# An encoder-layer kernel: start loads from two queues, two down tiles at once, another order of the last products, and some low weight parts added by transfer

## The chip, the cores and the metric

The kernel runs on one core of one Trainium2 chip. The metric is the device time of one execution in microseconds (us); before the change its median over three runs is 1635.33 us (1635.21 to 1636.85). The core has TensorE (PE in the profile; its weight loads are PEld), VectorE (DVE), ScalarE (ACT), GpSimd (POOL) and SyncE (SP); each works through its own queue of instructions in order.

## What is computed

One step of a streaming encoder layer for 512 prompt tokens and 64 sample tokens (576 in all), model width 1024, hidden width 2816:

```python
h = layer_norm(ALPHA * x + 0.5 * swiglu_ffn(x, p['ffn1_w_gu'], p['ffn1_w_down']), p['ln1_g'], p['ln1_b'])
mix, new_state = token_mixer(h, p, conv_prev, ml_state, att_past)
h = layer_norm(ALPHA * h + mix, p['ln2_g'], p['ln2_b'])
h = layer_norm(ALPHA * h + 0.5 * swiglu_ffn(h, p['ffn2_w_gu'], p['ffn2_w_down']), p['ln3_g'], p['ln3_b'])

def swiglu_ffn(x, w_gu, w_down):
    gate, up = jnp.split(x @ w_gu, 2, axis=-1)
    return (jax.nn.silu(gate) * up) @ w_down
```

The token mixer projects `h` by a wide `w_in` (among its columns attention's v, k and q, the first three taken), runs an mLSTM and a band attention, and merges both. All is float32.

## The kernel before, in words

**Split precision.** A float32 operand is split into a high part, which ACT writes by a copy that rounds (`act(hi, raw)`, line 137), and a low part, the rest, which DVE writes by a subtraction (`tt(lo, raw, f(hi), ALU.subtract)`, line 140). A product is three matmuls on PE (line 123): high by high, high by low, low by high. Weights come as tiles of 128 x 1024 (the third part of a down tile is 128 x 768).

**The weight pump.** `plan` (lines 287 to 312) lists every streamed weight tile in the order of use: first gate and up tiles `gu`, then the down tiles `dn` with three parts `c` each (`DC`: 8, 8 and 6 tiles of k), then `in` 48, 40 and 32, and so on. `pump` (line 171) loads the next tile into one of two buffers `wr` from SP's queue and splits the oldest into one of four pairs `wh`, `wl`. Some tiles next to the norms (`PIECES`, line 160) are split in two pieces of 512 columns, and of two of them (`ON_POOL`) the low part is subtracted on POOL.

**The start.** Lines 332 to 338 load the first three weight tiles in column pairs (`w0`), interleaved with the eight tiles of x, all from SP's queue; lines 367 to 376 split them in the same order: per pair of k three weight pieces and two pieces of x.

**A feed-forward part** (`ffn`, line 716). A few gate and up tiles run as plain products (`gemm`). The rest run two by two as units in the manner of Strassen (`Units`, line 582): seven products of four row blocks with combinations of the activations (`Combos.make`, line 554, buffers `tx`, `NX` of them, the rest from a common pool) and of the weights (`prep`, line 608). A unit's products are, in order: a11·b11, [the two last products of the unit before], a12·b21, s2·t2, s1·t1, s3·t3, then a22·t4 and s4·b22 within the next unit or, for the last, at the end (`run`, `finish`). Copies e1, e2, e3 of partial sums go to ACT, each ahead of the product that adds to the same bank. `tail` lets the pump go on to the down tiles; it is called between the two last products.

**The down projection** (lines 770 to 776). The 22 hidden tiles `h` are split as they are needed (`Hidden`), the first eleven into `hc`, the later ones into the left slots of `h`; `get` asks for four tiles ahead. Of eight output tiles j the first six run for both token halves together, one tile after the other; the last two run half by half. Each output tile goes to `Norm.cb`.

**The norms** (`Norm`, line 385) work by halves of the tokens. `stats` sums on PE, takes the variance on DVE and the power −1/2 on POOL (`rsqrt_cols`, line 380), makes a diagonal `dg` on DVE; `spread` multiplies it out on PE; `centre` subtracts the mean, six of eight tiles on DVE and two on POOL; `apply` scales on DVE, adds the bias on ACT and splits. Behind norm 1 stand the `in` tiles, behind norm 2 the `gu2` tiles, and in norm 1 POOL also splits the past of the attention's cache (`vc`, `kh`, `kl`).

A scheduler puts the instructions of each engine in one fixed order, by priorities (`hot`, `high_priority`) and by the program's order.

Of the kernel before, what the change touches and what calls it, by code (L numbers as in the profile page):

```python
# [81 lines left out]
def tile_layer(ctx: ExitStack, tc: tile.TileContext, ins, outs):  # L82
# [53 lines left out]
    def act(out, in_, func=AF.Copy, **kw):  # L136
        ACT.activation(out, in_, func, **kw)  # L137
# [18 lines left out]
    WARM = 8  # L156
    LAST = {1: 6, 2: 6}
    CL = {1: 2, 2: 3}
    NX = 10
    PIECES = {("gu2", 0, 0), ("gu2", 0, 1), ("gu2", 1, 0), ("gu2", 1, 1), ("in", 48), ("in", 40), ("in", 32)}  # L160
    ON_POOL = {("gu2", 0, 0), ("gu2", 1, 0)}
    CP = (6, 7)
    CPF = (4, 5, 6, 7)
    GR = 450
# [5 lines left out]
    @hot(30)  # L170
    def pump(limit=2):
        while True:
            c = wst["conv"]
            if wst["dma"] < min(len(plan), c + 2):
                i = wst["dma"]
                raws[i] = wpool.tile([P, 1024], F32, tag="wr", name=nm("wr"), bufs=2)
                src = plan[i][1]
                SP.dma_start(raws[i][:, :src.shape[1]], src)
                wst["dma"] += 1
                continue  # L180
            if c < wst["stop"] and c < wst["taken"] + limit and c < wst["done"] + NWB:
                raw = raws.pop(c)
                n = plan[c][1].shape[1]
                hi = wpool.tile([P, 1024], F32R, tag="wh", name=nm("wh"), bufs=NWB)
                if plan[c][0] == "if":

                    r3 = raw[:, :n].rearrange("p (k c) -> p k c", c=64)
                    h3 = hi.rearrange("p (k c) -> p k c", c=P)
                    act(h3[:, :, 0:64], r3)
                    tt(h3[:, :, 64:128], r3, f(h3[:, :, 0:64]), ALU.subtract)  # L190
                    parts[c] = (hi, None)
                else:
                    lo = wpool.tile([P, 1024], F32R, tag="wl", name=nm("wl"), bufs=NWB)
                    step = n if plan[c][0] not in PIECES else 512
                    for a in range(0, n, step):
                        act(hi[:, a:a + step], raw[:, a:a + step])
                        tt(lo[:, a:a + step], raw[:, a:a + step], f(hi[:, a:a + step]), ALU.subtract,
                           POOL if plan[c][0] in ON_POOL else DVE)
                    parts[c] = (hi, lo)
                wst["conv"] += 1  # L200
                continue
            return
# [35 lines left out]
    def gemm(tiles, xs, cbs, passes=NORMAL, tags=None):  # L238
# [7 lines left out]
        for p, (tl, hl) in enumerate(passes):  # L246
# [27 lines left out]
            for t in tl:  # L274
                for hf in hl:
                    cbs[t](hf, pss[t, hf][:, :HALVES[hf][1]])

    def one(key):
        return [[(key, KT)]]

# [46 lines left out]
    def load_x(hf, k0):  # L327
        t0, n = HALVES[hf]
        for k in (k0, k0 + 1):
            SP.dma_start(xr[k][:, t0:t0 + n], ins["xT"][:, k, t0:t0 + n])  # L330

    for k0 in range(0, KT, 2):
        ww = slice(k0 * P, (k0 + 2) * P)
        SP.dma_start(w0[:, 0:3:2, ww], ins["w_gu1"][0:2, :, ww].rearrange("c p n -> p c n"))
        load_x(0, k0)
        SP.dma_start(w0[:, 1, ww], ins["w_gu1"][FT, :, ww])
    for k0 in range(0, KT, 2):
        load_x(1, k0)
# [204 lines left out]
    class Combos:  # L543
# [6 lines left out]
        def tile(self):  # L550
            self.n += 1
            return slot(F32R, self.pool, "tx", bufs=NX) if self.n <= NX else slot(F32R)

        def make(self, i):
            k1, k2 = 4 + i, i
            r1, r2 = self.raw[k1], self.raw[k2]
            a, b = slice(0, HT_), slice(HT_, T)
            (h1, l1), (h2, l2) = self.xs.p[k1], self.xs.p[k2]
            d = self.b[i] = {"b11": (h1[:, a], l1[:, a]), "b21": (h2[:, a], l2[:, a]), "b22": (h2[:, b], l2[:, b])}
            tmp = self.pool.tile([P, 2, HT_], F32, tag="tt", name=nm("tt"), bufs=1)  # L560
            u, v = tmp[:, 0, :], tmp[:, 1, :]
# [12 lines left out]
            out("t1", u, -1.0, ha[:, a], la[:, a])  # L574
            out("t3", v, 1.0, ha[:, b], la[:, b])
            hb, lb = self.tile(), self.tile()
            tt(v, r2[:, b], u, ALU.subtract)
            out("t2", v, -1.0, hb[:, a], lb[:, a])
            tt(u, v, r2[:, a], ALU.subtract)
            out("t4", u, 1.0, hb[:, b], lb[:, b])  # L580

    class Units:


        def __init__(self, n, j0, hr, pool, combos):
            self.w, self.hr, self.pool, self.x = ins[f"w_gu{n}"], hr, pool, combos
            self.raw, self.ws, self.p = {}, {}, {}
            self.js = list(range(j0, FT))

        def load(self, j):  # L590
            if j >= FT:
                return
            w = self.raw[j] = self.pool.tile([P, 2048], F32, tag="wu", name=nm("wu"), bufs=2)
            SP.dma_start(w[:, 0:1024], self.w[j])
            SP.dma_start(w[:, 1024:2048], self.w[FT + j])

        def parts(self, src, small=False):
            n = 512 if small else 1024
            if small:
                hi, lo = (self.pool.tile([P, 512], F32R, tag=t, name=nm(t), bufs=1) for t in ("ah", "al"))  # L600
# [7 lines left out]
        def prep(self, j, what):  # L608
# [3 lines left out]
            if what == "a":  # L612
                p["a12"], p["a11"] = self.parts(w[:, 0:1024])
            elif what == "s":
                q = self.pool.tile([P, 2, 512], F32, tag="ws", name=nm("ws"), bufs=1)
                r = self.pool.tile([P, 2, 512], F32, tag="wt", name=nm("wt"), bufs=1)
# [28 lines left out]
        def run(self, tail):  # L645
            cur = None
            for j in self.js + [None]:
# [4 lines left out]
                    with tc.high_priority(offset=60):  # L652
                        new["E1"] = self.copy(new["X"], "e1", 1)
                if cur is not None:
                    self.finish(cur, j, tail)
# [24 lines left out]
        def finish(self, u, nxt, tail):  # L680
# [6 lines left out]
            if nxt is None:  # L687
                tail()
# [7 lines left out]
    class Hidden(Act):  # L696
# [6 lines left out]
        def upto(self, k):  # L703
            while len(self.p) <= min(k, FT - 1):
                j = len(self.p)
                pool, tag = self.pools[j >= FT // 2]
                hi, lo = (pool.tile([P, T], F32R, tag=tag, name=nm(tag), bufs=FT + (tag == "h")) for _ in range(2))
# [7 lines left out]

    def ffn(xs, n, gi, raw, final=None, prev=None):
        hh = {}
        with tc.tile_pool(name=nm("hr"), bufs=FT, side="right", reuse_waits="tile") as hr:

            def gate_cb(j):  # L720
                def cb(hf, ps):
# [17 lines left out]
            with tc.tile_pool(name=nm("sx"), bufs=1, side="right", reuse_waits="tile") as sx:  # L739
                combos = Combos(xs, raw, sx)  # L740
                un = Units(n, CL[n], hr, sx, combos)
                un.hr_done = hh.__setitem__
                j0 = CL[n]
                un.load(j0)
                un.load(j0 + 1)
# [21 lines left out]
            if final is not None:  # L767

                HALVES[:], BLOCKS[:] = HALVES_[1], BLOCKS_[1]
            with tc.tile_pool(name=nm("hc"), bufs=FT, side="right", reuse_waits="tile") as hc:  # L770
# [756 lines left out]
```

## Time and profile before

| | before |
|---|---|
| median of 3 runs | 1635.33 us (1635.21 to 1636.85) |
| profiled execution | 1635.94 us |
| its span | 1634.2 us |
| mean clock granted to TensorE | 0.988 |
| PE busy | 98% of the span |
| DVE, ACT, POOL busy | 67%, 50%, 9% |
| moved by DMA | 146.51 MB, 90 GB/s on the mean |

How to read the rows that follow: a row of a timeline has the start, the time, the engine, the line of the kernel, the operation, output and input tiles, shape, the count of instructions put together, and in brackets the idle time before it with what ended it. A row of waits has the total, the count and the longest. A row of windows has a stretch of the span, its length, and the busy time of each engine within it, then the clock granted to TensorE (1.00 is full), the busy share of the DMA engines and GB/s. A row of DMA issues ends with the us from issue to landing.

### The profile page before, as it was taken

How to read it: one execution, taken by the hardware profiler on the slowest of the kernel's cores; microseconds unless marked ns; L12 is line 12 of the kernel's file. 1: busy time of each engine (PE TensorE's matmuls, PEld its weight loads, DVE VectorE, ACT ScalarE, POOL GpSimd, SP SyncE). 2: the span in 40 equal slices, each digit the busy share in tenths (PEclk: the TensorE clock that was granted, in tenths of full speed). 3: DMA queues.
4: the chain of work that ended last, by engine and by line, in shares of the span. 5: the costliest groups of instructions: out<-in, count | busy, mean ns of one | idle time of the engine just before them, and what ended most of it. 6: DMA issues, size and time to landing. Idle time of an engine off the chain costs nothing.

```text
span 1634.2 us, 29320 instructions
## 1 busy us (share of the span) xinstructions
PE 1593.3 (98%) x11831; PEld 1567.2 (96%) x11831; DVE 1090.1 (67%) x2158; ACT 811.2 (50%) x1529; POOL 141.1 (9%) x277
## 2 busy tenths in 40 slices
PE   8999998999999999999999999999999999999997
PEld 8999998999999999999999999999999999998996
DVE  7777777535788777673656748434778777768336
ACT  6445546223566566651657466443345554545223
POOL 0000000000313323000111101002020000000001
PEclk9999999999999999999999999999989999999999
DMA  6222221224342333122222122222212222212333
GB/s 215 73 83 104 93 89 48 82 84 119 120 135 89 100 106 101 48 85 85 78 72 78 59 94 67 68 78 78 83 62 103 104 83 100 104 62 59 87 93 116
DMA packets 52320, 146.51 MB, mean 90 GB/s; under 512 B 5720, under 2 KB 16600, under 8 KB 52184
## 3 DMA queue, kind: packets, MB, share of 16 engines
q1 hardware_dynamic: 52184, 144.63, 27.3%
q8 instruction: 93, 1.52, 0.4%
q14 instruction: 43, 0.35, 0.1%
HBM read 135.37 MB, written 9.24 MB: 88 GB/s over the span
## 4 chain that ended last, share of the span: by engine, by line
PE 56%; DVE 3%; issue 1%; ACT 1%; POOL 1%; ACTq 0%; POOLq 0%; DVEq 0%
PE mm L123 51%; PE aux L123 4%; PE aux L133 1%; DVE s L140 1%; DVE h L140 0%; ACT s L137 0%; DVE wl L140 0%; DVE hc L140 0%; POOL wl L140 0%; POOL kh L147 0%; DVE s L143 0%; DVE ptl L140 0%; ACT sc L137 0%; ACT L137 0%; POOL rs L382 0%
## 5 line engine op out<-in xcount | busy, mean ns | idle before, releaser
L123 PE MATMUL mm<-s,wh 128*128 128x256 f32 (+2 forms) x3872 | 796.0, 299 | 11.4 <-ACT s L137 9.3
L123 PEld LDWEIGHTS mm<-s,wh 128*128 128x128 f32 x3872 | 624.9, 190 | 16.4 <-ACT s L137 10.1
L123 PE MATMUL mm<-s,wl 128*128 128x256 f32 (+2 forms) x1920 | 569.1, 296 | 0.0
L123 PEld LDWEIGHTS mm<-s,wl 128*128 128x128 f32 x1920 | 365.0, 190 | 0.0
L140 DVE TENSOR_TENSOR wl<-wr,wh 128x1024 fp32r<-128x1024 f32 (+2 forms) x166 | 195.9, 1183 | 186.4 <-ACT wh L137 185.8
L137 ACT ACTIVATE wh<-wr 128x1024 fp32r<-128x1024 f32 (+2 forms) x171 | 169.7, 996 | 301.5 <-PE mm L123 281.6
L123 PE MATMUL mm<-hc,wh 128*128 128x256 f32 (+1 forms) x704 | 147.7, 301 | 9.8 <-DVE hc L140 5.8
L123 PE MATMUL mm<-h,wh 128*128 128x256 f32 (+1 forms) x704 | 140.7, 294 | 0.0
L123 PEld LDWEIGHTS mm<-hc,wh 128*128 128x128 f32 x704 | 116.4, 192 | 13.2 <-DVE hc L140 8.9
L123 PE MATMUL mm<-tx,wh 128*128 128x288 f32 x624 | 128.3, 296 | 0.0
L140 DVE TENSOR_TENSOR wl<-ws,wh 128x1024 fp32r<-128x1024 f32 x39 | 47.8, 1226 | 111.1 <-ACT wh L137 111.1
L123 PEld LDWEIGHTS mm<-h,wh 128*128 128x128 f32 x704 | 112.7, 187 | 0.2
L123 PE MATMUL mm<-hc,wl 128*128 128x256 f32 (+1 forms) x352 | 105.1, 299 | 0.0
L123 PE MATMUL mm<-h,wl 128*128 128x256 f32 (+1 forms) x352 | 103.3, 294 | 0.0
L123 PEld LDWEIGHTS mm<-tx,wh 128*128 128x128 f32 x624 | 100.9, 190 | 0.0
L123 PE MATMUL mm<-tx,wl 128*128 128x288 f32 x312 | 92.8, 297 | 0.0
L137 ACT ACTIVATE wh<-ws 128x1024 fp32r<-128x1024 f32 x39 | 41.3, 1058 | 102.4 <-PE mm L123 101.7
L382 POOL TENSOR_TENSOR rs<-var,mhalf 128x2 f32<-128x2 f32 (+1 forms) x6 | 5.2, 865 | 825.0 <-DVE var L143 425.0
L123 PEld LDWEIGHTS mm<-hc,wl 128*128 128x128 f32 x352 | 67.7, 192 | 0.0
L123 PEld LDWEIGHTS mm<-h,wl 128*128 128x128 f32 x352 | 65.9, 187 | 0.0
L137 ACT ACT_TABLE_LOAD x45 | 57.7, 1283 | 5.5 <-DVE U L143 4.0
L123 PEld LDWEIGHTS mm<-tx,wl 128*128 128x128 f32 x312 | 59.1, 190 | 0.0
(282 smaller groups left out, 2864.3 us busy)
## 6 DMA issues: line engine op xcount, KB each, us to landing
wu<-in_w_gu SPq DMA_DIRECT2D x78, 512.0 KB, 4.3
wr<-in_w_in SPq DMA_DIRECT2D x72, 512.0 KB, 3.5
wr<-in_w_dn SPq DMA_DIRECT2D x40, 512.0 KB, 3.5
wr<-in_w_dn SPq DMA_DIRECT2D x20, 384.0 KB, 3.2
G<-in_rbias SPq DMA_DIRECT2D x16, 256.0 KB, 2.9
wr<-in_w_ap SPq DMA_DIRECT2D x8, 512.0 KB, 3.5
wr<-in_w_mp SPq DMA_DIRECT2D x8, 512.0 KB, 3.5
wr<-in_w_o SPq DMA_DIRECT2D x8, 512.0 KB, 3.5
```

The source lines that it names most:

```text
L123: PE.matmul(out, lhsT, rhs, start=start, stop=stop, **kw)
L133: PE.transpose(out, in_, idn)
L137: ACT.activation(out, in_, func, **kw)
L140: return (eng or DVE).tensor_tensor(out, a, b, op=op)
L382: return y, POOL.tensor_tensor(y, v, mhalf[:, :n], op=ALU.pow)
```

## The change

Four things are changed.

1. **First loads.** The tiles of x for k 0 to 3, first half, are loaded from ACT's queue; SP's queue keeps the rest.
2. **Two down tiles side by side.** The new `joined` runs output tiles 0 and 1 together over all k, their sums in two kinds of banks; the plan puts their parts in that order. The split of hidden tile 0 goes to buffers of its own (`h0`) and is asked for when unit 8 is done (the scheduler may place it earlier); its place in `hc` is given back, and seven more are asked for at the start. Weight buffers of the units are in a pool of their own (`sw`), so that the order of release fits.
3. **Order of the last products.** In the last unit a12·b21 (`first`) comes after s3·t3, ahead of a22·t4; `tail` is called where a12·b21 used to be. `make` gets priority 80 and `NX` is 8.
4. **Added by transfer.** For the tiles in `ADDED` (the six `gu2` tiles, `in` 48, 40, 32, and the six parts of the first two down tiles of both feed-forward parts: 21 in all) the low part is no longer a subtraction on DVE or POOL: ACT writes −hi into `lo`, and a DMA issued from POOL's queue reads the raw tile from memory once more and adds it to `lo`. The pieces of 512 columns are gone.

```diff
-    NX = 10
-    PIECES = {("gu2", 0, 0), ("gu2", 0, 1), ("gu2", 1, 0), ("gu2", 1, 1), ("in", 48), ("in", 40), ("in", 32)}
-    ON_POOL = {("gu2", 0, 0), ("gu2", 1, 0)}
+    NX = 8
+    NH0 = 1
+    ADDED = {(f"gu2", j, e) for j in range(3) for e in range(2)} | {("in", 48), ("in", 40), ("in", 32)} \
+        | {(f"dn{n}", j, c) for n in (1, 2) for j in range(2) for c in range(3)}
...
-                    step = n if plan[c][0] not in PIECES else 512
-                    for a in range(0, n, step):
-                        act(hi[:, a:a + step], raw[:, a:a + step])
-                        tt(lo[:, a:a + step], raw[:, a:a + step], f(hi[:, a:a + step]), ALU.subtract,
-                           POOL if plan[c][0] in ON_POOL else DVE)
+                    act(hi[:, :n], raw[:, :n])
+                    if plan[c][0] in ADDED:
+                        act(lo[:, :n], f(hi[:, :n]), scale=-1.0)
+                        POOL.dma_start(lo[:, :n], plan[c][1], accum_op=ALU.add)
+                    else:
+                        tt(lo[:, :n], raw[:, :n], f(hi[:, :n]), ALU.subtract)
...
+    def joined(keys, xs, cbs):
+        pss = {(t, hf): bank("mm" if t == 0 else "aux")[:, :HALVES[hf][1]] for t in range(2) for hf in range(2)}
+        last = len(DC) - 1
+        for c, ts_ in [(c, (0, 1)) for c in range(last)] + [(last, (0,)), (last, (1,))]:
+            ids = {t: take(keys[t][c]) for t in ts_}
+            k0, nk = DC[c]
+            for i in range(nk):
+                ww = slice(i * P, (i + 1) * P)
+                st, sp = k0 + i == 0, c == last and i == nk - 1
+                for t in ts_:
+                    wh, wl = parts[ids[t]]
+                    for hf in range(2):
+                        xh, xl = xs.get(k0 + i, hf)
+                        mm(pss[t, hf], wh[:, ww], hs(xh, hf), st, False)
+                        mm(pss[t, hf], wh[:, ww], hs(xl, hf), False, False)
+                        mm(pss[t, hf], wl[:, ww], hs(xh, hf), False, sp)
+                        od.tick()
...
-        for j in (*range(KT), *range(LAST[n], KT)):
-            for c, (k0, nk) in enumerate(DC):
-                plan.append(((f"dn{n}", j, c), ins[f"w_dn{n}"][j][:, k0 * P:(k0 + nk) * P]))
+        order = [(j, c) for c in range(3) for j in range(2)]
+        order += [(j, c) for j in (*range(2, KT), *range(LAST[n], KT)) for c in range(3)]
...
-        load_x(0, k0)
+        load_x(0, k0, ACT if k0 < 4 else SP)
...
+        @hot(80)
         def make(self, i):
...
-                Y = bank("mm")[:, :HT_]
-                self.product(Y, j, "a12", "b21", True, True)
-                with tc.high_priority(offset=60):
-                    tt(h[:, :HT_], Y, new["E1"], ALU.add)
-                    act(h[:, :HT_], h[:, :HT_], AF.Silu)
+                def first(new=new, j=j, h=h):
+                    Y = bank("mm")[:, :HT_]
+                    self.product(Y, j, "a12", "b21", True, True)
+                    with tc.high_priority(offset=60):
+                        tt(h[:, :HT_], Y, new["E1"], ALU.add)
+                        act(h[:, :HT_], h[:, :HT_], AF.Silu)
+                if j < FT - 1:
+                    first()
+                else:
+                    tail()
...
+                if j == FT - 1:
+                    first()
...
+                def hr_done(j, h):
+                    hh[j] = h
+                    if j == 8:
+                        hp_.upto(NH0 - 1)
...
-                hp_ = Hidden(hh, ((hc, "hc"), (hr, "h")))
-                hp_.upto(5)
+                hp_.pools[1] = (hc, "hc", FT - 2 * NH0)
+                hp_.spare = slot(F32R, hc, "hc", bufs=FT - 2 * NH0)
+                hp_.upto(7)
...
-                for j, hl in [(j, (0, 1)) for j in range(LAST[n])] + [(j, (hf,)) for hf in (0, 1) for j in range(LAST[n], KT)]:
+                joined([[(f"dn{n}", j, c) for c in range(3)] for j in range(2)], hp_, [ln.cb(j) for j in range(2)])
+                for j, hl in [(j, (0, 1)) for j in range(2, LAST[n])] + [(j, (hf,)) for hf in (0, 1) for j in range(LAST[n], KT)]:
```

More of the change, by code (lines that the diff above doesn't have):

```diff
@@ L276, in gemm @@
                     cbs[t](hf, pss[t, hf][:, :HALVES[hf][1]])
+    def joined(keys, xs, cbs):
[15 more added lines that the diff above has]
+                        od.tick()
+            for t in ts_:
+                done(ids[t])
+                if c == last:
+                    for hf in range(2):
+                        cbs[t](hf, pss[t, hf])
     def one(key):
@@ L291, in plan_ffn @@
         stops.append(len(plan))
-        for j in (*range(KT), *range(LAST[n], KT)):
-            for c, (k0, nk) in enumerate(DC):
-                plan.append(((f"dn{n}", j, c), ins[f"w_dn{n}"][j][:, k0 * P:(k0 + nk) * P]))
+        order = [(j, c) for c in range(3) for j in range(2)]
+        order += [(j, c) for j in (*range(2, KT), *range(LAST[n], KT)) for c in range(3)]
+        for j, c in order:
+            k0, nk = DC[c]
+            plan.append(((f"dn{n}", j, c), ins[f"w_dn{n}"][j][:, k0 * P:(k0 + nk) * P]))
     def plan_in(cols_):
@@ L325, in tile_layer, with load_x @@
     wst["dma"] = wst["conv"] = 3
-    def load_x(hf, k0):
+    def load_x(hf, k0, eng):
         t0, n = HALVES[hf]
         for k in (k0, k0 + 1):
-            SP.dma_start(xr[k][:, t0:t0 + n], ins["xT"][:, k, t0:t0 + n])
+            eng.dma_start(xr[k][:, t0:t0 + n], ins["xT"][:, k, t0:t0 + n])
     for k0 in range(0, KT, 2):
@@ L334, in tile_layer @@
         SP.dma_start(w0[:, 0:3:2, ww], ins["w_gu1"][0:2, :, ww].rearrange("c p n -> p c n"))
-        load_x(0, k0)
+        load_x(0, k0, ACT if k0 < 4 else SP)
         SP.dma_start(w0[:, 1, ww], ins["w_gu1"][FT, :, ww])
     for k0 in range(0, KT, 2):
-        load_x(1, k0)
+        load_x(1, k0, SP)
     cols = const.tile([P, NCOL], F32, name="cols")
@@ L582, in tile_layer, with __init__ @@
     class Units:
-        def __init__(self, n, j0, hr, pool, combos):
-            self.w, self.hr, self.pool, self.x = ins[f"w_gu{n}"], hr, pool, combos
+        def __init__(self, n, j0, hr, pool, wp, combos):
+            self.w, self.hr, self.pool, self.wp, self.x = ins[f"w_gu{n}"], hr, pool, wp, combos
             self.raw, self.ws, self.p = {}, {}, {}
@@ L592, in load @@
                 return
-            w = self.raw[j] = self.pool.tile([P, 2048], F32, tag="wu", name=nm("wu"), bufs=2)
+            w = self.raw[j] = self.wp.tile([P, 2048], F32, tag="wu", name=nm("wu"), bufs=2)
             SP.dma_start(w[:, 0:1024], self.w[j])
@@ L599, in parts @@
             if small:
-                hi, lo = (self.pool.tile([P, 512], F32R, tag=t, name=nm(t), bufs=1) for t in ("ah", "al"))
+                hi, lo = (self.wp.tile([P, 512], F32R, tag=t, name=nm(t), bufs=1) for t in ("ah", "al"))
             else:
@@ L614, in prep @@
             elif what == "s":
-                q = self.pool.tile([P, 2, 512], F32, tag="ws", name=nm("ws"), bufs=1)
-                r = self.pool.tile([P, 2, 512], F32, tag="wt", name=nm("wt"), bufs=1)
+                q = self.wp.tile([P, 2, 512], F32, tag="ws", name=nm("ws"), bufs=1)
+                r = self.wp.tile([P, 2, 512], F32, tag="wt", name=nm("wt"), bufs=1)
                 tt(q, w[:, 512:1536].rearrange("p (a c) -> p a c", c=512),
@@ L654, in run @@
                 if cur is not None:
-                    self.finish(cur, j, tail)
+                    self.finish(cur)
                 if j is None:
@@ L677, in run, with finish @@
                 self.prep(j + 1, "u")
+                if j == FT - 1:
+                    first()
                 cur = new
-        def finish(self, u, nxt, tail):
+        def finish(self, u):
             j, h = u["j"], u["h"]
@@ L686, in finish @@
             self.load(j + 3)
-            if nxt is None:
-                tail()
             self.product(u["Z"], j, "s4", "b22", False, True)
@@ L705, in upto @@
                 j = len(self.p)
-                pool, tag = self.pools[j >= FT // 2]
-                hi, lo = (pool.tile([P, T], F32R, tag=tag, name=nm(tag), bufs=FT + (tag == "h")) for _ in range(2))
+                pool, tag, n = self.pools[(j >= NH0) + (j >= FT // 2)]
+                hi = pool.tile([P, T], F32R, tag=tag, name=nm(tag), bufs=n)
+                lo = self.spare if j == FT // 2 - 1 else pool.tile([P, T], F32R, tag=tag, name=nm(tag), bufs=n)
                 act(hi, self.raw[j])
@@ L717, in ffn @@
         hh = {}
-        with tc.tile_pool(name=nm("hr"), bufs=FT, side="right", reuse_waits="tile") as hr:
+        with tc.tile_pool(name=nm("hr"), bufs=FT, side="right", reuse_waits="tile") as hr, \
+                tc.tile_pool(name=nm("h0"), bufs=2 * NH0, side="right", reuse_waits="tile") as h0:
             def gate_cb(j):
@@ L738, in ffn @@
                 prev.close()
-            with tc.tile_pool(name=nm("sx"), bufs=1, side="right", reuse_waits="tile") as sx:
+            with tc.tile_pool(name=nm("sw"), bufs=1, side="right", reuse_waits="tile") as sw, \
+                    tc.tile_pool(name=nm("sx"), bufs=1, side="right", reuse_waits="tile") as sx:
                 combos = Combos(xs, raw, sx)
-                un = Units(n, CL[n], hr, sx, combos)
-                un.hr_done = hh.__setitem__
+                un = Units(n, CL[n], hr, sx, sw, combos)
+                hp_ = Hidden(hh, [(h0, "h0", 2 * NH0), None, (hr, "h", FT + 1)])
+                def hr_done(j, h):
+                    hh[j] = h
+                    if j == 8:
+                        hp_.upto(NH0 - 1)
+                un.hr_done = hr_done
                 j0 = CL[n]
@@ L769, in ffn @@
                 HALVES[:], BLOCKS[:] = HALVES_[1], BLOCKS_[1]
-            with tc.tile_pool(name=nm("hc"), bufs=FT, side="right", reuse_waits="tile") as hc:
-                hp_ = Hidden(hh, ((hc, "hc"), (hr, "h")))
-                hp_.upto(5)
+            with tc.tile_pool(name=nm("hc"), bufs=FT - 2 * NH0, side="right", reuse_waits="tile") as hc:
+                hp_.pools[1] = (hc, "hc", FT - 2 * NH0)
+                hp_.spare = slot(F32R, hc, "hc", bufs=FT - 2 * NH0)
+                hp_.upto(7)
                 ln = Norm(xs, 2.0 * ALPHA, 4.0 * EPS, gi, final)
-                for j, hl in [(j, (0, 1)) for j in range(LAST[n])] + [(j, (hf,)) for hf in (0, 1) for j in range(LAST[n], KT)]:
+                joined([[(f"dn{n}", j, c) for c in range(3)] for j in range(2)], hp_, [ln.cb(j) for j in range(2)])
+                for j, hl in [(j, (0, 1)) for j in range(2, LAST[n])] + [(j, (hf,)) for hf in (0, 1) for j in range(LAST[n], KT)]:
                     gemm([[((f"dn{n}", j, c), nk) for c, (_, nk) in enumerate(DC)]], hp_, [ln.cb(j)], (((0,), hl),))
```

## The prediction

> **What bounds the kernel now.** I read the page's busy times first, then PE's waits, then windows around the large idle spots (columns: stretch, length, busy time of PE, PEld, DVE, ACT, POOL with counts, PE clock, DMA share, GB/s).
>
> ```profile
> PE 1593.3 (98%) x11831; PEld 1567.2 (96%) x11831; DVE 1090.1 (67%) x2158; ACT 811.2 (50%) x1529; POOL 141.1 (9%) x277
> PE mm L123 <- ACT s L137: 9.3, 3, 5.3
> PE mm L123 <- DVE hc L140: 5.8, 11, 1.2
> 10.00:15.00 5.00, 4.96 (x22) 4.73 (x23) 4.74 (x14) 4.60 (x15) 0.00 (x0) 0.50 0.99 318
> 44.00:50.00 6.00, 4.75 (x22) 4.54 (x23) 2.42 (x5) 1.31 (x4) 0.00 (x0) 0.72 0.00 0
> 260.00:290.00 30.00, 24.30 (x151) 22.71 (x150) 21.13 (x31) 17.79 (x30) 0.00 (x0) 0.89 0.28 79
> 270.00:278.00 8.00, 6.74 (x28) 6.54 (x29) 7.89 (x13) 6.54 (x12) 0.00 (x0) 0.57 0.19 49
> 1208.00:1220.00 12.00, 11.22 (x51) 10.63 (x52) 8.67 (x20) 5.82 (x17) 2.69 (x3) 0.57 0.23 77
> 1460.00:1490.00 30.00, 23.62 (x151) 21.33 (x151) 22.48 (x33) 18.69 (x30) 0.00 (x0) 0.94 0.28 79
> 1471.00:1476.00 5.00, 3.42 (x14) 3.19 (x15) 4.90 (x8) 3.78 (x7) 0.00 (x0) 0.66 0.28 79
> ```
>
> TensorE works 98% of the span, in an order of matmuls that the change leaves as it is but for the two entries into the down projections. So a part pays or costs only where PE waits, and in the slow stretch behind a wait: each of the five short windows follows an idle of about 2 us or more. Busy time times (1 − clock) prices that stretch: 2.5 (start), 1.3, 2.9, 4.8, 1.2; mean 2.5. I charge **2.5 us of clock** for every new stall of 2 us or more, between 1.2 and 4.8.
>
> The two entries lose, idle plus clock: 30 − 24.30 + 2.9 = **8.6** in FFN1, 30 − 23.62 + 1.2 = **7.6** in FFN2.
>
> **Start (first loads from ACT's queue).**
>
> ```profile
> 8.96 0.72 ACT L137 ACTIVATE wh<-w 128x256 fp32r<-128x256 f32 x2 [0.37 <-DMA w<-in_w_gu]
> 10.04 1.10 PE L123 MATMUL mm<-s,wh 128*128 128x256 f32 x2 [5.26 <-ACT s L137]
> 4.62 0.43 SPq L334 DMA_DIRECT2D w<-in_w_gu  x1
> ```
>
> ACT works in order, so the first split of x stands behind eight weight splits, the last fed by the load issued at 4.62. Four x loads leave SP's queue for ACT's; that weight load can go about 1.1 us sooner. But the window above has DMA at 0.99, and the bytes ahead of the first matmul are the same. I take −0.8, between 0 (bandwidth decides) and −1.8. ACT's four extra issues lie ahead of data that has not landed. The Trainium skill (DMA: Bandwidth & Descriptors, its remarks on issuing engines) says that spreading loads over issuing engines adds no bandwidth and saves only issue time; by that rule the term would be 0, and the 0.99 agrees in part.
>
> **First Strassen unit (`make` hot, NX 8).**
>
> ```profile
> 44.62 0.40 PE L123 MATMUL mm<-s,wh 128*128 128x288 f32 x1 [2.03 <-ACT s L137]
> ```
>
> In the changed order of DVE's queue the last combinations stand a little sooner, but one 0.75 us split of `h` (row below) stands ahead of them. −0.5, between −1.5 and +0.75.
>
> **Entries into the down projections (`first`, `joined`, `h0`).**
>
> ```profile
> 264.68 0.53 PE L123 MATMUL mm<-tx,ah 128*128 128x288 f32 x2 [1.15 <-ACT e L137]
> 268.05 1.06 ACT L137 ACTIVATE wh<-wr 128x1024 fp32r<-128x1024 f32 x1 [3.42 <-PE mm L123]
> 269.01 0.43 ACT L137 ACTIVATE h<-h 128x288 f32<-128x288 f32 x1
> 269.34 1.81 ACT L137 ACTIVATE hc<-h 128x576 fp32r<-128x576 f32 x3
> 270.06 0.39 PE L123 MATMUL mm<-hc,wh 128*128 128x256 f32 x1 [1.92 <-ACT hc L137]
> 271.65 0.58 PE L123 MATMUL mm<-hc,wh 128*128 128x256 f32 x1 [1.20 <-DVE hc L140]
> 272.18 0.75 DVE L140 TENSOR_TENSOR h<-h,h 128x576 fp32r<-128x576 f32 x1
> 272.85 0.75 DVE L140 TENSOR_TENSOR hc<-h,hc 128x576 fp32r<-128x576 f32 x1
> ```
>
> Before, PE waits 1.15 for the copy e3, 1.92 for the first split of `h`, 1.20 for the next, and then runs at the splits' pace: two splits per k, 0.67 us apart (272.18 to 272.85), are 1.34, and one tile uses a k in 6 × 0.133 = 0.8 (the norm 1 rows below have 8 matmuls of 256 columns from 418.51 to 419.47, 0.12 each; with 288 on the mean 0.133). After, the a12·b21 product (12 matmuls, 1.6 us) comes between s3·t3 and a22·t4, so e3 has 1.6 us more: 1.15 gone. k=0 is split long before. Two tiles use a k in 1.6, more than 1.34: the pace stall is gone. A new one comes at k=1. With 0 at the end of s4·b22, ACT has in order, at starts 0.96 apart for a 1024-wide pass: wh of tile 1 (freed at −4.9), e3, its new −hi pass to −2.6, then three more 1024-wide passes, a silu (0.34) and the split of k=11 (a third of 1.81: 0.6) up to 0.25, then wh 0.25–1.2 (it waits for the last product), silu to 1.55, −hi to 2.5, and only then the split of k=1, ready at 3.2 with its low part at 3.9. PE wants it at 1.6: **2.2 us** of stall, plus 2.5 clock: 4.7. So 8.6 − 4.7 = −3.9 and 7.6 − 4.7 = −2.9, together **−6.8**. If the clock stays up it is −11.8.
>
> The low part of tile 1 is now made by a transfer that GpSimd issues after the −hi pass (−2.6) and that must land by 1.07. No such transfer is in the trace. Rows nearest to its size X:
>
> ```profile
> wu<-in_w_gu SPq DMA_DIRECT2D x78, 512.0 KB, 4.3
> G<-in_rbias SPq DMA_DIRECT2D x16, 256.0 KB, 2.9
> wu<-in_w_gu SPq DMA_DIRECT2D x1, 512.0 KB, 7.6
> ```
>
> I take **X = 4.3** (the 512 KB row with company), since this one also reads its target and GpSimd has to make the request; bounds 2.9 (half the bytes) and 7.6 (the same load in the crowded start). The k=1 stall hides it up to X = 5.3. The Trainium skill (DMA: Bandwidth & Descriptors, "Anatomy of one DMA — SWDGE (gpsimd) path") fits 2.0 us plus bytes over 436 GB/s: 3.2 us as an estimate. By that figure both norms below would be 1.1 us cheaper each; no run here shows it yet.
>
> **Norm 1 (in 48, 40, 32).**
>
> ```profile
> 410.57 0.63 ACT L137 ACTIVATE wh<-wr 128x512 fp32r<-128x512 f32 x1 [1.53 <-DMA wr<-in_w_in]
> 414.94 1.31 ACT L137 ACTIVATE s<-s,cols 128x256 fp32r<-128x256 f32 x3 [0.44 <-DVE s L143]
> 418.51 0.40 PE L123 MATMUL mm<-s,wh 128*128 128x256 f32 x2
> 419.47 0.28 PE L123 MATMUL mm<-s,wl 128*128 128x256 f32 x1
> 420.93 0.83 PE L123 MATMUL aux<-onec,s 128*128 128x1 f32 x6 [0.46 <-DVE s L140]
> 423.55 1.04 POOL L382 TENSOR_TENSOR rs<-var,mhalf 128x3 f32<-128x3 f32 x1 [4.20 <-DVE var L143]
> 424.62 1.10 DVE L140 TENSOR_TENSOR dg<-ident,rs 128x256 f32<-128x256 f32 x1 [0.75 <-POOL rs L382]
> 426.43 1.13 POOL L147 TENSOR_SCALAR vc<-vp 128x128 fp32r<-128x128 f32 x2
> 433.38 0.40 POOL L147 TENSOR_SCALAR kl<-kl 64x256 fp32r<-64x256 f32 x1
> 428.66 0.70 PE L123 MATMUL aux<-dg,one 128*128 128x320 f32 x2
> ```
>
> Here the added transfers stand in the open. From 410.57, when the first of the three weights lands, ACT now has three 1024-wide wh, three −hi (0.96 each), six scaled copies (about 0.40 each from the x3 row) and a square (0.4): 5.8 + 2.4 + 0.4 = 8.6, so the −hi of in 32 ends at 419.1. PE takes its low part in the third triple, at 419.47; it lands at 419.1 + 4.3 = 423.4: a stall of 3.9 (that of in 40, some 3 us earlier, is covered by it). Behind it on PE stand the sums of half 1 and everything later. An idle of 0.46 just after it in the trace goes: +3.4, with clock **+5.9**. Six DVE subtractions fall away here, on an engine that PE waited 0.46 for.
>
> A second wait hides under the first: the power of half 1 (423.55 before) now stands on GpSimd's queue behind vc, kh and kl, a chain of 433.8 − 426.4 = 7.4 us with its gaps. Started at about 423 when vp has landed, it ends near 430.4, the power near 431.4 and the diagonal (1.10 + 0.86) near 433.2, 4.5 us after the spread matmul's old 428.66. PE comes there at 428.66 + 5.9 = 434.6, so it costs nothing; with X at 2.9 it would keep the loss at about 4.
>
> **Norm 2 (six gu2 tiles).**
>
> ```profile
> 1197.38 0.42 DVE L140 TENSOR_TENSOR s<-s,c 128x256 f32<-128x256 f32 x1 [1.66 <-ACT c L137]
> 1202.55 1.15 ACT L137 ACTIVATE wh<-wr 128x512 fp32r<-128x512 f32 x2 [0.92 <-PE mm L123]
> 1202.99 3.27 DVE L140 TENSOR_TENSOR s<-s,c 128x256 f32<-128x256 f32 x3
> 1203.26 2.73 POOL L140 TENSOR_TENSOR wl<-wr,wh 128x512 fp32r<-128x512 f32 x2 [2.88 <-ACT wh L137]
> 1208.63 0.92 PE L123 MATMUL mm<-s,wh 128*128 128x256 f32 x2 [2.03 <-ACT s L137]
> ```
>
> GpSimd's subtractions go, and with them the slowing of DVE beside them (three centrings in 3.27 us, 0.42 each elsewhere). The normed half is ready near 1206.7 instead of 1208.6, so 1.8 of the 2.03 goes. But wh of gu2(1,0) cannot start before 1202.55 and its −hi, behind a square, ends near 1205.3; the low part lands at 1209.6, and is wanted in the third triple, at 1207.6: 2.0 of new stall. Before 2.03 + 4.8 clock, after 0.25 + 2.0 + 2.5: **−2.1** (from −6 to +3.5 over X).
>
> **Sum.** −0.8 − 0.5 − 6.8 + 5.9 − 2.1 = −4.3 against the profiled execution's 1635.94 (span 1634.2 and 1.7 around it). That execution lies 0.6 above the median, so the forecast median is **1631.0**. The other added transfers, and ACT's extra −hi passes for them, lie under PE work of 3 us and more per tile; uncovered, one costs its X.
>
> **The rivals.**
> *The added transfers are slow, and the kernel is slower.* Place: the low parts of in 32 and gu2(1,0). Each us of X above 4.3 costs one at either norm, and above 5.3 one at either entry. The gain is gone at X = 5.9, and at 7.6 it is 2 × 3.3 + 2 × 2.3 − 4.3 = +6.9: 1642. For it: the 7.6 row, DVE busy at both norms, and three transfers queued on one engine; against it: DMA share is 0.2 to 0.4 there. The Trainium skill (SBUF — State Buffer, the "DVE blocks DMA" trap) tells that requests made on GpSimd starve while DVE runs certain fast modes; that would push X up.
> *The waits are short and the clock stays.* X = 2.9, no slow stretch at the entries or norm 2: −0.8 − 0.5 − 11.8 + 4.0 − 6.0 = −15: 1620. For it: a 0.46 idle was not followed by a slow stretch; against it: each idle of 2 us was.
> *The entries don't gain.* If ACT's queue at k=1 is late by 3 us more, so that they keep their price, the sum is +2.5: 1637. For it: everything hangs on one ACT queue; against it: its rows add up to 3.2.
>
> **How the numbers follow.** Forecast 0.42 (own range 1627 to 1635), slow transfers 0.27, short waits 0.20, entries without gain 0.11. A measurement of this kernel tells 0.2% (3.3 us) from none: of the forecast half is faster by more, the rest within; of the slow case nearly all slower; of the short case all faster; of the last half within. Faster 0.43, within 0.27, slower 0.30. The range 1620 to 1641 leaves out the ends of the two outer cases.
>
> **What would show it.** After: PE waits for a transfer of `wl` of about 4 us near 419 and 2 us near 1207; the 1.92 and 1.20 waits at the entries replaced by one of about 2 at the second k; the issue-to-landing row of `wl` near 4.3. Wrong if that row is over 6 or under 3, if PE stalls on the diagonal in norm 1, or if the entries still lose 7 us or more.

## The result, and the profile after

The kernel became slower. The changed kernel takes 1652.42 us (median of 4 runs, 1647.79 to 1653.03) where the kernel before takes 1636.09 (4 runs, 1635.21 to 1636.99): a ratio of 1.0094, 95% interval 1.0074 to 1.0113. The forecast was 1631.0. The profiled execution is the shortest of the four, 1647.79 us with a span of 1646.0, 11.8 us over the span before; what the other three lose beyond it, the profile can't show.

The page's busy times, PE's waits (total, count, longest) and the DMA issues (last number: us from issue to landing) of the changed kernel:

```profile
PE 1592.8 (97%) x11831; PEld 1568.9 (95%) x11831; DVE 1065.2 (65%) x2134; ACT 828.8 (50%) x1543; POOL 153.0 (9%) x294
PE mm L123 <- DMA wl<-in_w_gu: 10.4, 3, 4.9
PE aux L123 <- DMA wl<-in_w_dn: 9.2, 2, 4.6
PE mm L123 <- DMA wl<-in_w_in: 7.5, 3, 4.4
wl<-in_w_dn POOLq DMA_DIRECT2D x8, 512.0 KB, 8.4
wl<-in_w_gu POOLq DMA_DIRECT2D x6, 512.0 KB, 7.2
wl<-in_w_in POOLq DMA_DIRECT2D x3, 512.0 KB, 6.2
DMA to landing us min/median/max: 5.0/7.2/9.2
```

PE does the same work (1592.8 us busy, 1593.3 before) and has a new kind of wait, for the added transfers: 27.1 us in eight waits. The waits for the splits `hc` (5.8 us for DVE's and 3.8 for ACT's before) are gone from the list. The transfers take 7.2 us on the median, not 4.3.

Where the time goes is read from instructions that both kernels have. The first four rows are of the kernel before: a copy in the last unit but one of FFN1, the means of the norms (first one in norm 1, last one in norm 3, by their start), the first product with the merged branches, and the copy of that unit in FFN2.

```profile
253.28 0.39 ACT L137 ACTIVATE e<-mm 128x288 f32<-128x288 f32 x1
L123 PE MATMUL aux<-s,ones_d x12: 379/462/881, 399.5 to 1622.4; 128*128 128x256 f32 x6, 128*128 128x320 f32 x6
L123 PE MATMUL mm<-mg,wh x224: 276/292/393, 1153.8 to 1202.2; 128*128 128x256 f32 x56, 128*128 128x320 f32 x56
1454.62 0.39 ACT L137 ACTIVATE e<-mm 128x288 f32<-128x288 f32 x1
```

The same four of the changed kernel:

```profile
251.81 0.39 ACT L137 ACTIVATE e<-mm 128x288 f32<-128x288 f32 x1
L123 PE MATMUL aux<-s,ones_d x12: 379/462/881, 394.4 to 1634.2; 128*128 128x256 f32 x6, 128*128 128x320 f32 x6
L123 PE MATMUL mm<-mg,wh x224: 276/294/393, 1160.5 to 1210.1; 128*128 128x256 f32 x56, 128*128 128x320 f32 x56
1470.63 0.39 ACT L137 ACTIVATE e<-mm 128x288 f32<-128x288 f32 x1
```

So the changed kernel is 1.5 us ahead before the entry of FFN1 (start and first unit), 5.1 ahead at the first mean of norm 1, 6.7 behind at the merged branches, 16.0 behind near the end of FFN2's units, and 11.8 behind at the last mean. In parts: −1.5, the first entry −3.6, then norm 1 +11.8, norm 2 with the `gu2` tiles behind it +9.3, and the second entry −4.2. Of the five terms of the forecast's sum three came out near their size; the two norms came out 21.1 where it had +3.8.

The timeline of PE shows the waits. Norm 1 has one at each of the three low parts (first three rows), norm 2 two, gu2(2,0) one, and the first entry one:

```profile
414.12 0.39 PE L123 MATMUL mm<-s,wl 128*128 128x256 f32 x1 [0.39 <-DMA wl<-in_w_in]
417.42 0.58 PE L123 MATMUL mm<-s,wl 128*128 128x256 f32 x1 [2.69 <-DMA wl<-in_w_in]
422.86 0.58 PE L123 MATMUL mm<-s,wl 128*128 128x256 f32 x1 [4.43 <-DMA wl<-in_w_in]
1217.94 0.38 PE L123 MATMUL mm<-s,wl 128*128 128x256 f32 x1 [2.77 <-DMA wl<-in_w_gu]
1221.29 0.58 PE L123 MATMUL mm<-s,wl 128*128 128x256 f32 x1 [2.73 <-DMA wl<-in_w_gu]
1257.68 0.58 PE L123 MATMUL mm<-s,wl 128*128 128x256 f32 x1 [4.93 <-DMA wl<-in_w_gu]
270.91 0.58 PE L123 MATMUL aux<-h,wl 128*128 128x256 f32 x1 [4.65 <-DMA wl<-in_w_dn]
```

And on GpSimd's timeline, beside the −hi passes of ACT that they follow, stand the requests for the second and third of norm 1, for gu2(2,0) and (2,1), and for tile 1 of the first entry:

```profile
411.19 0.88 POOL L199 DMA_DIRECT2D wl<-in_w_in  x1 [1.80 <-ACT wl L137]
414.42 0.87 POOL L199 DMA_DIRECT2D wl<-in_w_in  x1 [2.36 <-DMA wr<-in_w_if]
1251.22 1.81 POOL L199 DMA_DIRECT2D wl<-in_w_gu  x2 [19.43 <-ACT wl L137]
262.99 0.87 POOL L199 DMA_DIRECT2D wl<-in_w_dn  x1 [3.69 <-ACT wl L137]
```

From request to first use that is 6.2, 8.4, 6.5 and 7.9 us. PE had less than that in hand at each. (The row at 414.42 names another transfer in its brackets; the −hi pass that it needs ended at 414.13, 0.3 us before.)

The windows around norm 1 (columns as before: stretch, length, busy PE, PEld, DVE, ACT, POOL, PE clock, DMA share, GB/s) show what comes with the waits:

```profile
414.00:418.00 4.00, 1.19 (x5) 1.00 (x6) 1.58 (x5) 1.12 (x3) 2.11 (x5) 0.93 0.99 256
418.00:422.00 4.00, 0.43 (x3) 0.13 (x1) 0.00 (x0) 0.00 (x0) 0.00 (x0) 0.50 1.01 221
422.00:426.00 4.00, 3.14 (x14) 3.14 (x15) 0.00 (x0) 0.00 (x0) 3.29 (x8) 0.50 0.72 272
426.00:430.00 4.00, 4.00 (x17) 3.61 (x17) 1.36 (x4) 0.61 (x2) 3.36 (x7) 0.50 0.12 38
430.00:434.00 4.00, 4.00 (x32) 4.00 (x31) 3.65 (x6) 0.00 (x0) 3.97 (x8) 0.87 0.00 0
1255.00:1262.00 7.00, 4.32 (x25) 4.32 (x26) 3.37 (x7) 1.24 (x4) 0.00 (x0) 0.76 0.94 261
```

The clock is at 0.50 from 418 to 430, far behind the last wait. That is some 4 us of clock (3.14 and 4.00 of work at half, 4.00 at 0.87) behind 7.5 us of waits. The last row is the stretch behind gu2(2,0): 4.32 at 0.76, 1.0 us of clock. The DMA engines are at 0.99 to 1.01 in the two windows in which PE waits most: the added transfers keep them full at 221 to 256 GB/s together with the loads beside them.

### The profile page after: what moved, and what is told of

The parts are those of the page before. It is cut to its first block, busy times and chain, and to the rows that moved or that the text cites. A ratio compares the mean times of both kernels' runs of the same rounds, so it can differ in the third digit from the quotient of the medians.

```text
span 1646.0 us, 29361 instructions
## 1 busy us (share of the span) xinstructions
PE 1592.8 (97%) x11831; PEld 1568.9 (95%) x11831; DVE 1065.2 (65%) x2134; ACT 828.8 (50%) x1543; POOL 153.0 (9%) x294
## 4 chain that ended last, share of the span: by engine, by line
PE 55%; issue 2%; DMA 2%; DVE 1%; ACT 1%; POOL 1%; ACTq 0%; SPq 0%; POOLq 0%
PE mm L123 48%; PE aux L123 5%; PE aux L133 1%; DMA wl<-in_w_gu 1%; DMA wl<-in_w_dn 0%; DMA wu<-in_w_gu 0%; ACT s L137 0%; ACT wh L137 0%; DVE s L140 0%; DVE wl L140 0%; POOL s L140 0%; DVE ptl L140 0%; ACT sc L137 0%; ACT L137 0%; POOL kh L147 0%
## 5 line engine op out<-in xcount | busy, mean ns | idle before, releaser
L123 PE MATMUL mm<-s,wh 128*128 128x320 f32 (+2 forms) x4028 | 829.1, 300 | 8.1 <-ACT s L137 6.1
L123 PEld LDWEIGHTS mm<-s,wh 128*128 128x128 f32 x4028 | 652.3, 191 | 12.5 <-ACT s L137 6.5
L123 PE MATMUL mm<-s,wl 128*128 128x320 f32 (+2 forms) x1998 | 594.3, 297 | 17.9 <-DMA wl<-in_w_gu 10.4
L137 ACT ACTIVATE wh<-wr 128x1024 fp32r<-128x1024 f32 (+1 forms) x164 | 168.5, 1031 | 288.1 <-PE mm L123 277.9
L140 DVE TENSOR_TENSOR wl<-wr,wh 128x1024 fp32r<-128x1024 f32 (+1 forms) x142 | 172.7, 1219 | 171.9 <-ACT wh L137 169.8
L123 PE MATMUL mm<-hc,wh 128*128 128x320 f32 (+1 forms) x560 | 113.4, 295 | 0.0
L123 PE MATMUL mm<-tx,wh 128*128 128x288 f32 x468 | 97.1, 296 | 0.0
L123 PEld LDWEIGHTS mm<-hc,wh 128*128 128x128 f32 x560 | 90.5, 189 | 0.0
L137 ACT ACTIVATE wh<-wu 128x1024 fp32r<-128x1024 f32 x39 | 41.4, 1062 | 34.8 <-PE mm L123 34.7
L137 ACT ACTIVATE e<-mm 128x288 f32<-128x288 f32 x117 | 47.3, 404 | 21.5 <-PE mm L123 21.5
```

The source lines that it names most:

```text
L123: PE.matmul(out, lhsT, rhs, start=start, stop=stop, **kw)
L140: return (eng or DVE).tensor_tensor(out, a, b, op=op)
```

## The experiments

Each time stands beside the median of the kernel before that was measured with it. These medians lie between 1635.84 and 1636.70, so a difference between versions that were measured at different times is uncertain by about 1 us.

**e1, the tiles next to the norms by subtraction.** `ADDED` has only the down tiles; the others are split as in the kernel before:

```diff
-    ADDED = {(f"gu2", j, e) for j in range(3) for e in range(2)} | {("in", 48), ("in", 40), ("in", 32)} \
-        | {(f"dn{n}", j, c) for n in (1, 2) for j in range(2) for c in range(3)}
+    PIECES = {("gu2", 0, 0), ("gu2", 0, 1), ("gu2", 1, 0), ("gu2", 1, 1), ("in", 48), ("in", 40), ("in", 32)}
+    ON_POOL = {("gu2", 0, 0), ("gu2", 1, 0)}
+    ADDED = {(f"dn{n}", j, c) for n in (1, 2) for j in range(2) for c in range(3)}
```

> The changed kernel, but the nine weight tiles next to the norms (in 48, 40, 32 and the gu2 tiles) have their low parts subtracted in pieces again, as in the kernel before; the down tiles are still added by transfer. Theory: the added transfers next to the norms land 5 to 9 us after they are issued and cost some 21 us there (PE waits for DMA wl of 7.5 and 10.4 us plus the slow clock behind them), while start and entries gain some 9: 1624 to 1631 us, no PE wait for DMA wl left but those of the down tiles. Rival (the loss comes from the side-by-side tiles, the order of the last products or the memory layout): still over 1642.

1626.48 us (1625.83 to 1629.41; before 1636.70, ratio 0.9946, 0.9928 to 0.9964). Of the transfers, PE waits only for those of the down tiles:

```profile
PE aux L123 <- DMA wl<-in_w_dn: 10.0, 2, 5.2
PE mm L123 <- ACT s L137: 8.2, 4, 4.4
```

Its span is 1624.0, 22 below the changed kernel's. The nine tiles next to the norms carry the whole loss: with their low parts subtracted, the change gains 10.2.

**e2, the down tiles by subtraction.** `ADDED` has only the nine tiles next to the norms.

> The changed kernel, but the twelve down tiles have their low parts subtracted on DVE; the tiles next to the norms are still added by transfer. Theory: the two waits of 4.6 us at the entries go and ACT loses four passes ahead of k=1, so that at most 2 us of stall is left at each: 5 to 9 us below the changed kernel of the same job. Rival (DVE is the limit at the entries and the transfers relieve it): not faster than the changed kernel, with waits for DVE wl or hc of over 4 us at each entry.

1646.57 us (1644.23 to 1646.72; before 1636.70, ratio 1.0066, 1.0047 to 1.0085), 5.9 below the changed kernel's median; the span is 3.5 lower. The waits for `wl` at the entries give way to 1.46 us for the split of k=1 and 0.97 for its low part. Against the medians the step is within the expectation, against the spans it is smaller. The rival's waits of over 4 us for DVE are not there.

**e3, nothing added.** Both edits together.

> The changed kernel without any added transfer: all low parts subtracted as before, pieces next to the norms. Start, order of the last products, side-by-side tiles and layout stay. Theory: both savings together, 1617 to 1626 us, entries that lose 3 us each or less. Rival (side-by-side tiles need the transfers): over 1630, with the loss at the entries at 7 us or more.

1622.11 us (1621.26 to 1623.45; before 1636.70, ratio 0.9917, 0.9900 to 0.9933). The two entries in windows and on PE's timeline:

```profile
255.00:285.00 30.00, 27.57 (x196) 27.08 (x195) 23.69 (x35) 20.60 (x32) 0.00 (x0) 0.94 0.24 66
1450.00:1480.00 30.00, 27.60 (x206) 27.14 (x205) 24.43 (x36) 20.89 (x33) 0.00 (x0) 1.00 0.23 66
268.19 0.39 PE L123 MATMUL mm<-hc,wh 128*128 128x256 f32 x1 [1.47 <-ACT hc L137]
269.54 0.58 PE L123 MATMUL mm<-hc,wh 128*128 128x256 f32 x1 [0.97 <-DVE hc L140]
```

Each entry now idles 2.4 us, where the kernel before idled 5.7 and 6.4; the stretch at 0.94 adds 1.7 at the first; the second, with waits of nearly the same length (1.46 and 0.94), has none. The side-by-side tiles don't need the transfers; they are better without.

**e4, the kernel before with the nine tiles added by transfer, and nothing else of the change.**

> The kernel before with one part of the change: the nine tiles next to the norms added by transfer. Theory: the whole loss shows by itself, 1650 to 1662 us, with PE waits for DMA wl at norm 1, norm 2 and gu2(2,0). Rival (the loss needs the other parts, for example an earlier arrival of PE at norm 1): 1633 to 1641.

1658.14 us (1656.28 to 1659.49; before 1636.70, ratio 1.0135, 1.0117 to 1.0154). PE waits for `wl` 10.2 us behind norm 2 and 8.0 in norm 1. The loss, 21.4 us, comes without any other part of the change.

**e5, a plain transfer in place of the added one.**

```diff
-                        POOL.dma_start(lo[:, :n], plan[c][1], accum_op=ALU.add)
+                        POOL.dma_start(lo[:, :n], plan[c][1])
```

> The changed kernel, but the 21 transfers from GpSimd's queue write the raw tile into the low part instead of adding it to -hi (the low part of these tiles is then the whole weight). Theory A (the adding makes them slow: its packets took 3.5 to 4 us for 512 KB where a plain load of that size lands in 3.5 us altogether): landing falls to 5 us or less on the median, each wait for DMA wl is 2 us or more shorter, the span 10 us or more below 1646. Theory B (the request made by GpSimd makes them slow): landing stays over 6.5 us, the span within 4 us of 1646.

The kernel leaves out the adding, and its low parts are not the right ones. It ran once: 1635.73 us, span 1633.9. The queue, the bytes, the count of requests and the waits for −hi are the same:

```profile
wl<-in_w_dn POOLq DMA_DIRECT2D x8, 512.0 KB, 5.2
wl<-in_w_gu POOLq DMA_DIRECT2D x6, 512.0 KB, 4.7
wl<-in_w_in POOLq DMA_DIRECT2D x3, 512.0 KB, 3.9
DMA to landing us min/median/max: 3.8/4.9/6.9
262.73 0.54 POOL L199 DMA_DIRECT2D wl<-in_w_dn  x1 [4.01 <-ACT wl L137]
```

Adding costs 2.3 us of landing (7.2 against 4.9 on the median) and a longer request on GpSimd (0.87 against 0.54). The two pages show where some of it lies. The packets of this queue, as many and with as many bytes, took 3.6% of the DMA engines' time with the adding and 2.1% without (the changed kernel, then e5):

```profile
q0 software_dynamic: 3024, 10.49, 3.6%
q0 software_dynamic: 3024, 10.49, 2.1%
```

PE still waits 17.3 us for the plain transfers, since they too begin only after −hi. The waits fell by 9.8 in all, so by less than the 2 each that theory A had; the span fell by 12.1. It is still 14.1 above e3's (1619.8): of the 26.2 by which the changed kernel lies above e3, more than half stays with plain transfers.

**e7, e3 with one queue at the start.** `load_x(0, k0, SP)` for all k.

> No added transfer (as in e3), and the first loads of x from SP's queue again. Theory: the first matmul of the layer comes at 10.0 instead of 9.47 us and nothing else changes: 0.3 to 1 us slower than e3. Rival (the two queues change nothing, since DMA is full): the first matmul within 0.2 us of e3's.

1620.93 us (1617.95 to 1623.96; before 1636.31); first matmul at 9.67, in e3 at 9.47. In the time the second queue gives nothing that shows within the spread of the runs. At the first matmul one pair of traces doesn't settle it: the ten traces with two queues have it at 9.15 to 9.85, the three with one queue (before, e4, e7) at 9.67 to 10.19.

**e8, e3 with output tiles 0 and 1 one after the other.** The call of `joined` and its order in the plan are taken out.

> No added transfer (as in e3), and output tiles 0 and 1 of the down projections one after the other again; the order of the last products, the early split of hidden tile 0 and the start stay. Theory: the pace of the splits (1.34 us for the two of a k, against 0.8 us in which PE uses a k of one tile) comes back: PE waits for hc of 4 us or more in each entry, 4 to 9 us slower than e3. Rival (the gain is that of the order of the last products and the early split): within 1.5 us of e3.

1630.34 us (1628.94 to 1631.86; before 1636.31, ratio 0.9965, 0.9952 to 0.9978), 8.2 above e3.

```profile
PE mm L123 <- DVE hc L140: 6.3, 15, 1.0
PE mm L123 <- ACT hc L137: 4.2, 2, 2.2
```

15 waits of PE for DVE's `hc` are back (two in e3): the pace of the splits, as the prediction read it. The side-by-side tiles make more than half of what e3 gains (8.2 of 14.6 us).

**e9, e3 with gu2(1,0) subtracted on DVE.** `ON_POOL = {("gu2", 0, 0)}`.

> No added transfer (as in e3), and the low part of gu2(1,0) subtracted in pieces on DVE instead of GpSimd. Theory: in norm 2 the three centrings on DVE take 1.2 instead of 3.3 us once GpSimd doesn't work beside them, the wait of 2.0 us for the split s falls to about 1 us, the slow stretch behind it gets shorter: 0 to 6 us faster than e3. Rival (the two pieces, 0.7 us each, stand ahead of the half that PE waits for): 0 to 3 us slower.

1621.15 us (1619.51 to 1624.69; before 1636.31, ratio 0.9910, 0.9893 to 0.9927). The wait of 2.02 for the split becomes 0.96, but 0.48 and 1.87 for later low parts follow. It can't be told from e3 by its time.

**e11, e9 with one transfer that is early.** `ADDED = {("gu2", 0, 0)}`.

> e9 (nothing added) plus one added transfer, that of gu2(0,0), whose -hi is done some 12 us before PE wants the low part. Theory (a transfer costs only what of its 7 us is not covered by the time between -hi and the first use): within 2 us of e9 (1621), no PE wait for DMA wl. Rival (the transfer costs by its traffic, its ACT pass or GpSimd's request): 3 us or more slower.

1618.97 us (1617.50 to 1621.16; before 1635.84, ratio 0.9901, 0.9885 to 0.9918), no wait for a transfer.

```profile
wl<-in_w_gu POOLq DMA_DIRECT2D x1, 512.0 KB, 5.9
1181.66 1.07 POOL L200 DMA_DIRECT2D wl<-in_w_gu  x1 [34.03 <-ACT wl L137]
1201.08 0.86 PE L123 MATMUL mm<-s,wh 128*128 128x256 f32 x2 [0.98 <-ACT s L137]
```

Issued at 1181.66 for a use behind 1201.08, its 5.9 us cost nothing. This version beats both kernels, by 1% against the kernel before; against e9 it is not told apart.

**e12, e9 with gu2(2,0) and (2,1) added.**

> e9 plus the added transfers of gu2(2,0) and gu2(2,1) alone, which the prediction counted as hidden. Theory: -hi of gu2(2,0) is done some 2 us before its first use, so one wait of 4 to 5 us and a slow stretch behind it: 5 to 8 us slower than e9. Rival (in the changed kernel that wait is the tail of the queue of the four before it): 0 to 2 us slower.

1626.25 us (1624.00 to 1626.96; before 1635.84, ratio 0.9943, 0.9925 to 0.9960), 5.1 above e9.

```profile
PE mm L123 <- DMA wl<-in_w_gu: 4.6, 1, 4.6
```

The wait is there without the four transfers ahead of it, so it is no tail of their queue.

**e13, e9 with in 48, 40 and 32 added.**

> e9 plus the added transfers of in 48, 40 and 32 alone. Theory: norm 1 shows its whole loss, three waits of 7 to 8 us in all and a slow stretch of 10 to 14 us behind them at half clock: 11 to 14 us slower than e9. Rival (the price of the forecast: 3.4 us of wait and 2.5 us of clock): 5 to 7 us slower.

1632.80 us (1630.76 to 1637.17, 10 runs; before 1635.84, ratio 0.9987, 0.9976 to 0.9998), 11.6 above e9; the three waits make 8.0 us. PE's waits, and the window around norm 1:

```profile
PE mm L123 <- DMA wl<-in_w_in: 8.0, 3, 5.2
400.00:436.00 36.00, 27.97 (x167) 26.71 (x166) 16.29 (x37) 11.79 (x21) 14.56 (x28) 0.76 0.59 158
```

Norm 1 alone loses what the trace of the changed kernel gave it (11.8). The rest above 8.0 goes with the clock, 0.76 on the mean of the stretch (1.00 in e9).

## Why the prediction was wrong

The rival "the added transfers are slow" came true, which had a chance of 0.27. Point by point:

- **Start, −0.8.** The first matmul moved from 10.04 to 9.39, near the forecast. How much of it is the second queue's stays open: e7 against e3 has 0.2 us, less than the traces with the same start differ among themselves, and the time shows nothing. The Trainium skill's rule on issuing engines (DMA: Bandwidth & Descriptors, "Issuing engines are not separate DMA queues"), by which the term would be 0, agrees with the time of e7.
- **First unit, −0.5.** The wait of 2.03 became 1.38, one of 0.63 became 0.86. Too small to be tested by itself.
- **Entries, −6.8.** They gave −7.8 by the milestones (−3.6 and −4.2). Half of the mechanism was right: the waits for e3 and the pace of the splits are gone. The other half was not: the stall that was forecast at k=1 stood at k=0 and was for a transfer, 4.65 and 4.56, longer than the 2.2 named. Its cause is X. ACT's work came as forecast, with the −hi pass of tile 1 done 2.4 us ahead of the entry (262.68 against 265.07) and the split of k=1 ready 3.2 behind it; but the low part of tile 1 landed 7.9 after its request, where 5.3 would have been hidden. With no transfer (e3) the stall is at k=1, 1.47 + 0.97. That the total came out near is luck, of two errors that cancel. By the windows below a new entry loses 4.6 of idle and 1.5 of clock, 6.1 and not 4.7. So the old ones, with what was gained, lost about 10 each, and not the 8.6 and 7.6 that the prediction took from idle and clock. The last two rows, of the kernel before, show why: at the pace of the splits a k took 1.33 us, 0.5 more than the 0.8 in which PE can use it, and the idle time shown has 0.28 of that.

```profile
255.00:285.00 30.00, 25.35 (x181) 25.15 (x180) 17.07 (x28) 23.38 (x36) 3.65 (x4) 0.94 0.58 132
1475.00:1505.00 30.00, 25.44 (x183) 25.18 (x182) 16.21 (x27) 24.15 (x37) 3.76 (x5) 0.94 0.61 139
1480.36 0.41 PE L123 MATMUL mm<-hc,wh 128*128 128x320 f32 x1 [0.28 <-DVE hc L140]
1481.69 0.41 PE L123 MATMUL mm<-hc,wh 128*128 128x320 f32 x1 [0.28 <-DVE hc L140]
```

- **X = 4.3: here the prediction failed.** It took the row of a load from SP's queue, with company, to cover GpSimd's request and the reading of the target as well. Measured: 7.2 on the median, 5.0 to 9.2; e5 puts 2.3 of it on the adding. The estimate from the Trainium skill's fit (DMA: Bandwidth & Descriptors, "Anatomy of one DMA — SWDGE (gpsimd) path"), 3.2 us, was further off: plain transfers from this queue took 3.8 to 6.9. The upper bound, 7.6, was the nearer row, and the point from which the gain is gone, X = 5.9, stood in the text. Whether DVE's work holds up the requests, as the rival's rule of the Trainium skill (SBUF — State Buffer, the "DVE blocks DMA" trap) would have it, no run here shows. At the longest wait of norm 1 it isn't the whole cause: from 418 to 422 DVE is idle (0.00) and the DMA engines are full (1.01), and PE still waits.
- **Norm 1, +5.9.** It was 11.8. The place was right (the third triple, the −hi of in 32 behind three weight splits and six scaled copies). PE waited 7.5 in all, 0.39 and 2.69 at the first two low parts and 4.43 at the third, where a stall of 3.9 was forecast. The first two waits are no loss of their own, as the prediction had it: the third transfer sets when PE can go on, and it landed 8.4 us after its request. With 8.4 for X the prediction's own working gives 8.0. And the clock was charged 2.5 and cost about 4. The second wait, GpSimd's power of half 1, stayed hidden: it started at 428.69, 0.33 after its variance.
- **Norm 2, −2.1.** PE does no longer wait 2.03 for the split, as forecast, but 2.77 and 2.73 for two low parts, with the same slow clock as before (0.68 over 16 us in both kernels). And gu2(2,0), which the prediction had put among the transfers that "lie under PE work of 3 us and more per tile", cost a wait of 4.93 and 1.0 of clock: its request came 1.5 us before PE wanted it, and 3 us of PE work would not have hidden 6.5 either. This is the second step that failed, an overlap put at nothing without looking up the distance: even the forecast X of 4.3 would have left 2.8 us of wait. e12 shows that term alone: 5.1.

Summed, the norms were forecast at +3.8 and cost 21.1; e4 shows 21.4 by themselves. That is 17.3 us too little, and the other terms came 1.2 better than forecast: together the 16.1 us by which the span missed (+11.8 against −4.3). With 7.2 for X, the prediction's own sum gives +5.3. So the size of X makes 9.6 of the 16.1, and of the 6.5 that are left gu2(2,0) has 5.9. The median lies 4.6 above the profiled execution; where the other runs lost that stays open. A slip without weight: by the prediction's own words its chance of faster is 0.41, not 0.43.

## What to carry to other kernels

A transfer that stands between a split and its first use is paid for by its full time from request to landing, less what lies between the two; look up that distance for each tile before the subtraction is taken off an engine, as e11 and e12 show with a transfer requested 19 and 1 us ahead. When an operation is absent from the trace, let the forecast ask whether its sign survives the upper bound, and state that as the likeliest case when several tiles in a row hang on it. Where PE uses tiles faster than an engine splits them, running two output tiles side by side halves the pace that the splits must hold, and that alone was worth 8 us here.

## What the runs showed of the hardware

- A transfer of 512 KB that adds to its target took 5.6 to 9.2 us from the request on GpSimd to its landing (the 5.0 above is one of 384 KB), a plain one from the same queue 3.8 to 6.9. The two largest groups of loads of that size from SP's queue land in 3.5 and 4.4 on the median.
- The request of an adding transfer held GpSimd for 0.85 to 1.07 us, of a plain one for 0.53 to 0.73.
- Waits of 7.5 us in three pieces, with PE at work between them, halved the clock for some 13.6 us (the windows 414 to 434); two waits of 1.46 and 0.94 at the second entry of e3 left it at 1.00, and two of 1.47 and 0.97 at its first entry went with 0.94 over 30 us. So here the length of the waits alone didn't settle the price.
